# Weight operands of a decoder layer begin at 27 places in memory instead of one

## Chip, cores and metric

The kernel runs on one core of one Trainium2 chip. The metric is device time in microseconds (us) of one execution. A core has several engines that run side by side: TensorE (PE; its weight loads are listed apart as PEld) multiplies matrices, VectorE (DVE) and ScalarE (ACT) do elementwise work, GpSimd (POOL) does a little here, and SyncE (SP) issues the DMAs. They share the on-chip memory SBUF with 128 partitions; the matmuls accumulate in PSUM.

## What is computed

One layer of a decoder, 1024 tokens, width 1024, all in float32:

```python
mods = silu_c @ w_ada[l] + b_ada[l]          # shift, scale, gate for three sub-layers
h = modulate(x, sh1, sc1)
y = swiglu(h, ffn1_w_gate[l], ffn1_w_up[l], ffn1_w_down[l])
x = layer_norm(ALPHA * x + (1 + g1) * (MACARON * y), ln1_g[l], ln1_b[l])
h = modulate(x, sh2, sc2)
y = token_mix(h, w_in[l], b_forget[l], swa_sinks[l], grp_gain[l], w_out[l])
x = layer_norm(ALPHA * x + (1 + g2) * y, ln2_g[l], ln2_b[l])
h = modulate(x, sh3, sc3)
y = swiglu(h, ffn2_w_gate[l], ffn2_w_up[l], ffn2_w_down[l])
x = layer_norm(ALPHA * x + (1 + g3) * (MACARON * y), ln3_g[l], ln3_b[l])
```

`swiglu` is `(silu(h @ w_gate) * (h @ w_up)) @ w_down` with an inner width of 2816. `token_mix` projects `h`, runs eight heads of sliding-window attention (window 128) and eight heads of forgetting attention (a cumulative sum of log forget gates is added to the scores), normalises both groups and projects back.

## The kernel before

A float32 operand is split into a high part and the rest (`split`, lines 100 to 102: a copy on ACT, a subtraction on DVE), and a product is three matmuls: high x high, high x rest, rest x high (`mm3`, lines 106 to 108). Nearly all PE work runs through these lines, 128 x 128 weights against up to 512 moving columns. The large products are computed by blocks with seven products instead of eight (a Strassen-like scheme), so DVE also forms sums and differences of blocks.

The work goes in this order: a start that modulates the input and begins the first FFN (`start_ffn1`); gate and up products of the first FFN (`gate_up`, eleven groups `g` of 2 x 7 products, in the class `Seven`); its down projection (`down`, seven products of eleven steps each); value, query and key projections; sliding-window attention, then forgetting attention, with projections as filler between; the output projection; the second FFN with `gate_up` and `down` again. Vector work on the modulation vectors (`ada_mul`, line 122) is spread through the first `gate_up`.

SBUF is given out by rings. A ring has a tag, a number of slots and a slot size; a tile takes a free slot, and its first writer waits until the last reader of the slot's former tile has finished. Before the change:

```python
RING = dict(h=(14, 8192), z=(4, 4096), q=(4, 4096), w=(6, 4096), u=(6, 2048), t=(7, 2048), b=(2, 4096))
```

The number pairs are slots and bytes per partition. The tiles of concern:

- `w`: split operands, high part and rest side by side, 4096 bytes. In `gate_up` and in the q/k projection they are the weights (stationary operand); in `down` and in the output projection they are the moving operand, and in the later products of `down` both. Each value tile and each projected q/k tile is also put together in a `w` tile before it is stored.
- `t`: short-lived sums, 2048 bytes: the partial results of the seven products, the sums `s1`, `s2` of weight blocks (lines 265 and 266), the `T2` sums of `down` (line 416), the split scores of both attentions, and the small arrays of the cumulative sum (lines 815 to 842).
- `upper`: a constant 128 x 128 triangle, loaded once at the start (line 650) and used by a single matmul, the cumulative sum over tokens (line 826).
- `u`: pieces of weights as they are loaded; `h`, `z`, `q`: larger operands.

Every slot of these rings is a whole number of 512 bytes long. The weight slices in a tile are 512 bytes long, the rows of a moving operand 2048 bytes. The second value projection is different: its weights (`wv_load`, line 772 on ACT and 773 on DVE) lie as slices of 328 columns, 1312 bytes, in an `h` tile and are the moving operand of 328-wide matmuls; the first value projection has slices of 320 columns, 1280 bytes.

The program is written in one order; a planner then orders each engine's instructions by that priority, by their dependencies and by the slots that are free, before the program runs. Each engine carries out its list strictly in order, and so does the DMA queue of SP.

Of the kernel before, what the change touches and what calls it, by code (L numbers as in the profile page):

```python
# [14 lines left out]
P = 128  # L15
# [22 lines left out]
RATIO2 = 0.3  # L38


RING = dict(h=(14, 8192), z=(4, 4096), q=(4, 4096), w=(6, 4096), u=(6, 2048), t=(7, 2048), b=(2, 4096))
BANK = dict(mm=3, o=1, y=2, tp=2)


# [1 line left out]
def layer_kernel(ctx, tc, xT, x, c, adaT, adab, wg1, wu1, wd1, wqk, wv1, wv2, bf, sinks,  # L46
# [5 lines left out]
    V, A, G, T, DMA = nc.vector, nc.scalar, nc.gpsimd, nc.tensor, nc.sync  # L52

    sb = ctx.enter_context(tc.tile_pool(name="sb", bufs=1))
# [4 lines left out]
    def mk(pool, shape, dt, tag, bufs):  # L59
        uid[0] += 1  # L60
        return pool.tile(shape, dt, tag=tag, name=f"{tag}_{uid[0]}", bufs=bufs)

    def st(tag, shape, dt=F32):
        assert 4 * math.prod(shape[1:]) <= RING[tag][1], (tag, shape)
        return mk(sb, shape, dt, tag, RING[tag][0])

    def const(shape, name, dt=F32):
        return sb.tile(shape, dt, tag=name, name=name, bufs=1)
# [4 lines left out]
    def psum(tag):  # L73
        return mk(ps, [P, HT], F32, tag, BANK[tag])
# [3 lines left out]


    ident = const([P, P], "ident")  # L80
    upper = const([P, P], "upper")
    cmask = const([P, P], "cmask")
    ones = const([P, P], "ones")
    nhalf = const([P, 8], "nhalf")
# [28 lines left out]
    def htiles():  # L113

        return [st("h", [P, 4, HT], F32R) for _ in range(2)]

    silu = st("b", [P, D])

    def ada_mul(w, j):
# [5 lines left out]
    def ada_block(m, d):  # L125
        j = m * KD + d
        w = st("q", [P, D])
        DMA.dma_start(w, adaT[j * P:(j + 1) * P, :])
        ada_mul(w, j)
# [517 lines left out]
    ops1, wo1, a1 = start_ffn1()  # L647

    DMA.dma_start(ident, consts[0])
    DMA.dma_start(upper, consts[1])  # L650
    DMA.dma_start(cmask, consts[2])
    DMA.dma_start(lnc, lncol)
    DMA.dma_start(gaincol, gain)
# [132 lines left out]
    for hf in range(2):  # L786
        if hf:
            wpre.append(weight_all(wqk, order[0], "w"))
        for pz, (w, ncol) in enumerate(((wva, NV1), (wvb, NV2))):
            for k in range(4):  # L790
                t = hf * 4 + k
                p = psum("y" if hf + pz == 0 and k < 2 else "mm")
# [19 lines left out]
    def flat(t):  # L812
        return t.rearrange("p a b -> p (a b)")
# [8 lines left out]
    V.tensor_tensor(fl, fl, fa, ALU.subtract)  # L822
    V.tensor_scalar(fz, fz, 0.0, None, op0=ALU.min)
    V.tensor_tensor(fl, fz, fl, ALU.subtract)
    pc = psum("tp")
    T.matmul(pc[:, :64], upper, flat(fl), start=True, stop=True)
    V.tensor_copy(flat(fw), pc[:, :64])
# [649 lines left out]
```

## Time and profile before

| | |
|---|---|
| median of two runs | 1780.41 us (1780.15 to 1780.66) |
| the profiled execution | 1779.88 us |
| span from the first to the last instruction in it | 1778.1 us |
| mean granted TensorE clock | 0.997 |
| PE / DVE / ACT busy | 98% / 85% / 44% of the span |
| DMA | 303.44 MB, 171 GB/s over the span |

A page of the profile lists busy time per engine, the span in 40 slices, the DMA queues, the chain of work that ended last, and the costliest groups of instructions. A group's row reads: source line, engine, operation, what it writes and reads by tile names (buffer numbers left out), shapes and count; then busy time in us and the mean of one in ns; then how long the engine sat idle just before these instructions and what ended that. A row of the timeline has the start in us, the duration, the engine, the line and the operation. Matmuls overlap in the pipeline, so a matmul's own duration is longer than its share of PE; the distance between two starts is what one costs in an unbroken run. In a table of stretches each row gives the stretch, its length, then busy time and instruction count of PE, PEld, DVE, ACT and POOL as far as they occur, the granted clock, the DMA share and GB/s.

### The profile page before, as it was taken

Reading aid. Unit: us, or ns where it says so; the run is one execution under the profiler, and the core shown is the slowest. Engines: PE = TensorE matmul, PEld = TensorE weight load, DVE = VectorE, ACT = ScalarE, POOL = GpSimd, SP = SyncE. Lnnn points to the kernel's source line nnn. Section 1 sums busy time; section 2 is a strip of 40 time slices with the busy share of each in tenths; the row PEclk is TensorE's granted clock in tenths of the full one; section 3 lists DMA queues with packets and bytes.
Section 4 is the critical chain, followed back from the end, with each engine's and each line's share of the span. In section 5 each row is a group of like instructions: output and inputs, shape, how many; then the busy total and the mean of one; then the engine's idle time right before and its main releaser. Section 6 shows DMA issues by size and latency. Waiting matters only on the chain.

```text
span 1778.1 us, 23525 instructions
## 1 busy us (share of the span) xinstructions
PE 1739.8 (98%) x8114; PEld 1435.1 (81%) x8114; DVE 1510.3 (85%) x2748; ACT 782.6 (44%) x1492; POOL 21.9 (1%) x32
## 2 busy tenths in 40 slices
PE   6999999999999999999999999999999999999997
PEld 5788888888888889887787768788888888888885
DVE  7999999999895788267787987998887887899688
ACT  5433333333444453277666651643333333354472
POOL 0000000000000000000000000000000000000000
PEclk9999999999999999999999999999999999999999
DMA  9355555556944327655767863243233232593452
GB/s 367 115 192 196 181 201 192 177 185 222 331 145 142 109 87 239 205 155 169 214 202 226 238 218 137 84 142 125 90 132 105 95 106 96 209 318 102 136 166 78
DMA packets 147047, 303.44 MB, mean 171 GB/s; under 512 B 15384, under 2 KB 29296, under 8 KB 146928
## 3 DMA queue, kind: packets, MB, share of 16 engines
q1 hardware_dynamic: 146928, 301.94, 52.3%
q8 instruction: 64, 1.05, 0.3%
q14 instruction: 55, 0.45, 0.1%
HBM read 224.17 MB, written 77.71 MB: 170 GB/s over the span
## 4 chain that ended last, share of the span: by engine, by line
PE 87%; DVE 8%; ACT 3%; issue 1%; POOL 0%; DMA 0%; SPq 0%; POOLq 0%; ACTq 0%; DVEq 0%
PE y L106 12%; PE y L107 12%; PE y L108 12%; PE mm L108 9%; PE mm L107 9%; PE mm L106 9%; PE o L106 3%; PE o L108 3%; PE o L107 3%; PE tp L106 2%; PE tp L107 2%; PE tp L108 2%; DVE h L102 2%; PE tp L1166 2%; PE o L1174 1%
## 5 line engine op out<-in xcount | busy, mean ns | idle before, releaser
L101 ACT CAST w<-u 128x512 fp32r<-128x512 f32 x295 | 181.4, 621 | 359.7 <-PE y L108 137.5
L106 PE MATMUL y<-h,w 128*128 128x512 f32 x716 | 281.4, 393 | 0.3 <-ACT w L101 0.3
L107 PE MATMUL y<-h,w 128*128 128x512 f32 x716 | 280.3, 391 | 0.0
L108 PE MATMUL y<-h,w 128*128 128x512 f32 x716 | 280.1, 391 | 0.0
L106 PE MATMUL mm<-h,w 128*128 128x512 f32 x540 | 211.3, 392 | 16.5 <-ACT h L101 15.7
L102 DVE TENSOR_TENSOR w<-u,w 128x512 fp32r<-128x512 f32 x295 | 200.9, 686 | 21.2 <-ACT w L101 20.3
L107 PE MATMUL mm<-h,w 128*128 128x512 f32 x540 | 211.7, 393 | 0.0
L108 PE MATMUL mm<-h,w 128*128 128x512 f32 x540 | 211.1, 392 | 0.4 <-DVE w L102 0.4
L106 PEld LDWEIGHTS y<-h,w 128*128 128x128 f32 x716 | 134.6, 188 | 27.5 <-ACT w L101 1.1
L108 PEld LDWEIGHTS y<-h,w 128*128 128x128 f32 x716 | 134.5, 188 | 25.7
L107 PEld LDWEIGHTS y<-h,w 128*128 128x128 f32 x716 | 134.6, 188 | 25.7
L101 ACT CAST w<-t 128x512 fp32r<-128x512 f32 x106 | 65.6, 620 | 174.5 <-PE mm L108 70.8
L106 PEld LDWEIGHTS mm<-h,w 128*128 128x128 f32 x540 | 101.7, 188 | 38.8 <-ACT h L101 16.1
L107 PEld LDWEIGHTS mm<-h,w 128*128 128x128 f32 x540 | 102.1, 189 | 21.8 <-DVE h L102 0.8
L108 PEld LDWEIGHTS mm<-h,w 128*128 128x128 f32 x540 | 102.1, 189 | 21.9 <-DVE w L102 1.1
L101 ACT CAST z<-u 128x512 fp32r<-128x512 f32 x88 | 54.8, 622 | 103.8 <-PE y L108 79.9
L102 DVE TENSOR_TENSOR t<-tp,t 128x512 fp32r<-128x512 f32 (+1 forms) x126 | 72.8, 586 | 20.0 <-ACT t L101 18.9
L102 DVE TENSOR_TENSOR z<-u,z 128x512 fp32r<-128x512 f32 x88 | 59.9, 687 | 26.6 <-ACT z L101 26.6
L101 ACT CAST w<-h 128x512 fp32r<-128x512 f32 x111 | 68.5, 617 | 31.8 <-DMA h<-in_wd 11.6
L102 DVE TENSOR_TENSOR w<-h,w 128x512 fp32r<-128x512 f32 x111 | 76.1, 686 | 5.0 <-ACT w L101 4.9
L101 ACT CAST t<-tp 128x512 fp32r<-128x512 f32 (+1 forms) x126 | 62.5, 501 | 32.6 <-PE tp L1166 31.7
L102 DVE TENSOR_TENSOR w<-t,w 128x512 fp32r<-128x512 f32 x106 | 72.6, 688 | 1.3 <-ACT w L101 0.8
(349 smaller groups left out, 3907.7 us busy)
## 6 DMA issues: line engine op xcount, KB each, us to landing
u<-aT SPq DMA_DIRECT2D x154, 256.0 KB, 2.8
q<-in_adaT SPq DMA_DIRECT2D x56, 512.0 KB, 3.4
u<-in_wg SPq DMA_DIRECT2D x92, 256.0 KB, 3.3
u<-in_wu SPq DMA_DIRECT2D x90, 256.0 KB, 2.8
aT<-z SPq DMA_DIRECT2D x44, 512.0 KB, 3.2
h<-in_wd SPq DMA_DIRECT2D x88, 256.0 KB, 5.4
qkd<-w SPq DMA_DIRECT2D x26, 512.0 KB, 3.7
aT<-b SPq DMA_DIRECT2D x22, 512.0 KB, 4.0
```

The source lines that it names most:

```text
L101: A.copy(hi, src)
L102: V.tensor_tensor(lo, src, hi.bitcast(F32), ALU.subtract)
L106: T.matmul(o, lh, rh, start=start, stop=False, skip_group_check=more)
L107: T.matmul(o, lh, rl, start=False, stop=False, skip_group_check=more)
L108: T.matmul(o, ll, rh, start=False, stop=stop, skip_group_check=more)
L1166: T.transpose(pt[:, tok(i - q0)], sps[i][:, tok(j)], ident)
L1174: T.matmul(po[:, c0:], vt, ph[:, c0:], start=j == 0, stop=False)
```

## The change

- The slots of ring `w` become 416 bytes longer (4512), and each new `w` tile starts 16 bytes further in its slot than the one before, from 0 to 416 bytes, after which it begins again: 27 places.
- Ring `t` has six slots instead of seven.
- The constant `upper` no longer has a place of its own. It becomes a tile of ring `t`, loaded just before the matmul that uses it.

```diff
-RING = dict(h=(14, 8192), z=(4, 4096), q=(4, 4096), w=(6, 4096), u=(6, 2048), t=(7, 2048), b=(2, 4096))
+RING = dict(h=(14, 8192), z=(4, 4096), q=(4, 4096), w=(6, 4096 + 416), u=(6, 2048), t=(6, 2048), b=(2, 4096))
...
+    turn = [0]
+
     def st(tag, shape, dt=F32):
-        assert 4 * math.prod(shape[1:]) <= RING[tag][1], (tag, shape)
-        return mk(sb, shape, dt, tag, RING[tag][0])
+        n = math.prod(shape[1:])
+        assert 4 * n <= RING[tag][1], (tag, shape)
+        if tag != "w":
+            return mk(sb, shape, dt, tag, RING[tag][0])
+
+        w = mk(sb, [P, RING[tag][1] // 4], dt, tag, RING[tag][0])
+        o = 4 * (turn[0] % 27)
+        turn[0] += 1
+        w = w[:, o:o + n]
+        if len(shape) == 3:
+            return w.rearrange("p (a b) -> p a b", a=shape[1])
+        return w.rearrange("p (a b c) -> p a b c", a=shape[1], b=shape[2]) if len(shape) == 4 else w
...
-    upper = const([P, P], "upper")
...
-    DMA.dma_start(upper, consts[1])
...
     V.tensor_tensor(fl, fz, fl, ALU.subtract)
+    upper = st("t", [P, P])
+    DMA.dma_start(upper, consts[1])
     pc = psum("tp")
     T.matmul(pc[:, :64], upper, flat(fl), start=True, stop=True)
```

## The prediction

> **What bounds the kernel now.** I read the page first: how busy the engines are, and the chain that ended last.
>
> ```profile
> span 1778.1 us, 23525 instructions
> PE 1739.8 (98%) x8114; PEld 1435.1 (81%) x8114; DVE 1510.3 (85%) x2748; ACT 782.6 (44%) x1492; POOL 21.9 (1%) x32
> PE 87%; DVE 8%; ACT 3%; issue 1%; POOL 0%; DMA 0%; SPq 0%; POOLq 0%; ACTq 0%; DVEq 0%
> ```
>
> TensorE (PE) carries 87% of the chain, so almost nothing but its own pace and its own waits can move the end. A mean hides stages, so I took the busy time by stretches (length, then busy PE, PEld, DVE, ACT with instruction counts, granted clock, DMA), and PE's waits.
>
> ```profile
> 80.00:200.00 120.00, 120.00 (x530) 98.81 (x530) 117.95 (x195) 38.98 (x67) 0.00 (x0) 1.00 0.57 194
> 200.00:340.00 140.00, 140.00 (x620) 115.81 (x619) 137.16 (x227) 44.59 (x76) 0.00 (x0) 1.00 0.55 187
> 340.00:380.00 40.00, 40.00 (x178) 33.14 (x177) 38.75 (x65) 12.34 (x21) 0.00 (x0) 1.00 0.60 193
> ...
> 760.00:860.00 100.00, 98.98 (x533) 78.62 (x532) 75.01 (x216) 73.92 (x221) 0.96 (x1) 1.00 0.58 167
> 860.00:1060.00 200.00, 193.92 (x1033) 154.40 (x1032) 171.21 (x438) 129.79 (x288) 1.65 (x1) 1.00 0.74 219
> 1060.00:1140.00 80.00, 78.78 (x379) 64.22 (x377) 65.04 (x109) 27.09 (x42) 6.74 (x9) 1.00 0.39 136
> ```
>
> ```profile
> PE mm L106 <- ACT h L101: 15.7, 2, 13.0
> PE y L106 <- ACT w L101: 1.8, 2, 1.5
> PE mm L1141 <- DVE s_mneg L1144: 1.6, 3, 0.6
> ```
>
> See two things. In the gate/up products of the first FFN (80 to 380 us) PE never idles, at full clock, and VectorE (DVE) is busy 293.9 of 300 us: it has 6.1 us to spare and would be the next bound. In the attention and output projection (760 to 1140) PE idles 1.0 + 6.1 + 1.2 = 8.3 us. The 13.0 us wait is the kernel's start; the other waits are for operands just computed, 1.8 us or less a pair.
>
> **The pace of PE.** Start times of matmuls inside unbroken runs, 512, 320 and 328 columns wide:
>
> ```profile
> 299.62 0.39 PE L107 MATMUL mm<-h,w 128*128 128x512 f32 x1
> ...
> 305.97 0.39 PE L108 MATMUL o<-h,w 128*128 128x512 f32 x1
> ```
> ```profile
> 699.82 0.31 PE L107 MATMUL mm<-h,h 128*128 128x320 f32 x1
> ...
> 705.98 0.31 PE L107 MATMUL mm<-h,h 128*128 128x320 f32 x1
> ```
> ```profile
> 711.77 0.31 PE L107 MATMUL mm<-h,h 128*128 128x328 f32 x1
> ...
> 719.84 0.31 PE L107 MATMUL mm<-h,h 128*128 128x328 f32 x1
> ```
>
> The first pair spans 28 steps: 6.35/28 = 226.8 ns a matmul. The second spans 42: 6.16/42 = 146.7 ns. The third spans 54: 8.07/54 = 149.4 ns. Widths 512 and 320 differ by 80.1 ns over 192 columns, 0.417 ns a column; that leaves 226.8 - 512 x 0.417 = 13.2 ns per matmul that doesn't grow with the columns. This 13.2 ns is all that a better place in memory could win, if operands at like places are what costs it.
>
> **Part 1, the places of `w`.** Nothing is computed differently: a `w` tile starts 0 to 416 bytes later in its slot, and the slots lie 4512 instead of 4096 bytes apart. How many instructions touch these tiles (busy PE, PEld, DVE, ACT, with counts):
>
> ```profile
> 0.00:1778.10 1778.10, 1431.14 (x6084) 1137.37 (x6084) 370.44 (x554) 331.62 (x554) 1.00 0.53 171
> ```
>
> So 6084 of 8114 matmuls read `w`, as weights or as the moving operand, and 554 operations each of DVE and ScalarE (ACT) write or read it. Do places matter to PE? Before, all slots of the wide rings and all slices in them lie a multiple of 256 bytes apart, with one exception: the slices of the second value projection are 328 x 4 = 1312 bytes apart, so its moving operand begins at 0, 288, 64, 352, 128 and 416 bytes past a multiple of 512, while its weights stay put. These are six of the 27 places, all multiples of 32. On the line through the other two widths a 328-wide matmul takes 13.2 + 328 x 0.417 = 150.0 ns; measured 149.4. So places 32 bytes apart change the pace by -0.6 ns, not by 13. 14 of the 27 places are multiples of 32. The other 13 are odd multiples of 16, and no row shows one; nor does a row show weights, rather than the moving operand, at other places. I bound an operation at an odd place by the whole of the 13.2 ns, gained or lost, and take 0 ns, being nearest to the 328-wide row; over 6084 matmuls the row's own -0.6 ns would be -3.7 us, which I keep for the range.
>
> DVE and ACT: the same 320- and 328-wide slices are written by these two groups (min/median/max).
>
> ```profile
> L773 DVE TENSOR_TENSOR h<-u,h x16: 489/491/501, 652.1 to 674.8; 128x320 fp32r<-128x320 f32 x8, 128x328 fp32r<-128x328 f32 x8
> ```
> ```profile
> L772 ACT CAST h<-u x16: 447/460/469, 651.2 to 674.3; 128x320 fp32r<-128x320 f32 x8, 128x328 fp32r<-128x328 f32 x8
> ```
> ```profile
> L102 DVE TENSOR_TENSOR w<-u,w 128x512 fp32r<-128x512 f32 x295 | 200.9, 686 | 21.2 <-ACT w L101 20.3
> ```
>
> A DVE column costs (686 - 491)/192 = 1.0 ns, so eight more columns are 8 of the 12 ns between least and most; 4 ns are left for the place. In the one stretch where DVE is near its limit about 110 operations write `w` (300 us / 38.1 us a group of 14 products x 14 splits): 110 x 4 ns = 0.4 us of the 6.1 spare. Cost 0. If that cover were gone, all of it would show.
>
> **Part 2, six slots for `t`.** A slot fewer matters only where seven sums live at once. Followed from first writer to last reader through the timeline, at most five live at once in the gate/up and attention stages, so six slots hold them with no new wait. Seven live only in the third product of the down projection, where DVE makes the T2 sums (L416) ahead of their splits:
>
> ```profile
> 1605.95 0.68 DVE L416 TENSOR_TENSOR t<-h,h 128x512 f32<-128x512 f32 x1
> ...
> 1614.38 0.68 DVE L416 TENSOR_TENSOR t<-h 128x512 f32<-128x512 f32 x1
> ...
> 1618.58 1.29 DVE L102 TENSOR_TENSOR w<-t,w 128x512 fp32r<-128x512 f32 x2
> ...
> 1631.83 0.69 DVE L102 TENSOR_TENSOR w<-t,w 128x512 fp32r<-128x512 f32 x1
> ```
> ```profile
> 1615.32 0.39 PE L106 MATMUL tp<-w,z 128*128 128x512 f32 x1
> ```
>
> The last T2 sum starts at 1614.4, its split at 1631.8, and six others are alive between. With six slots about ten sums (five in each down projection) must start 2 to 5.5 us later, after a split. What queues behind is DVE's own next split, and PE waits for that. PE starts this product at 1615.3 and needs a group each 12 x 226.8 = 2.7 us, so the fifth group at 1626.2; its split is done at about 1619.2. The lead is 7 us, more than 5.5. DVE has the same work in another order: 0, at worst the few us by which a lead is used up.
>
> **Part 3, the matrix `upper`.** Its 64 KB load leaves the start (0.42 us of the SP queue) and comes back just before the cumulative sum.
>
> ```profile
> L826 PE MATMUL tp<-t,upper x2: 217/245/273, 727.7 to 727.7; 128*128 128x64 f32 x2
> L650 SPq DMA_DIRECT2D upper<-in_consts x1: 423/423/423, 40.9 to 40.9; - x1
> DMA to landing us min/median/max: 5.3/5.3/5.3
> ```
> ```profile
> 723.11 0.36 SPq L801 DMA_DIRECT2D vd<-w  x1
> 723.83 1.08 SPq L558 DMA_DIRECT2D u<-in_wqk  x2
> 726.05 1.33 SPq L889 DMA_DIRECT2D h<-vd  x2
> ```
>
> The start gains nothing: PE's 13 us there wait for the first splits, long before 40.9. At 727.7 a late load would hold PE, with the q/k projection queued behind. The load waits for no data, only for a `t` slot, few of which are in use there, and SP's issues leave gaps (one ends at 723.47, the next begins at 723.83). If it is issued early it costs 0; if only with the chain at 724 to 726, at a landing of 5.3 us, 1.6 to 3.6 us. I take 0.5 us, near the early end, and keep 5.3 for the range. It pushes weight loads (L558) and `h<-vd` back by 0.42 us, hidden behind running matmuls.
>
> **Sum.** 1779.88 us (the profiled execution; span 1778.1 plus 1.8 around it) + 0 + 0 + 0.5 = 1780.4; the median of the runs is 0.5 above that execution, so **1781 us**. Below: -3.7 for places, -8.3 if another order of the attention stage removed all of PE's idle time: 1768. Above: +5.3 for `upper`, +8.3 if that idle time doubled: 1795. That order may shift at all, since slots decide when an instruction may be placed.
>
> **Rivals.**
> A, *the like places are the 13.2 ns.* For it: every matmul with `w` pays it, and all these operands begin at like places. Against: the 328-wide row. If odd places alone escape, 13/27 x 6084 x 13.2 ns = 39 us: 1742. If all do, 80 us: 1700. The Trainium skill ("TensorE: Matmul & The Clock Gate", section "Back-to-back issue gap") gives a warm gap of N/2.4 + 2.5 ns, 215.8 for 512 columns; the trace's 226.8 disagrees by 11 ns, and were the place the reason for all of it, that page would give 67 us less, about 1714. Chance 5%.
> B, *odd places cost PE a second fixed part.* The same 39 us the other way: 1820. Nothing in the trace speaks for it. The skill ("SBUF — State Buffer", section "Specifications (TRN2)") has lines of 16 bytes; by that page a start at a whole line touches no further line, which speaks against B, and no run shows it yet. Chance 3%.
> C, *DVE becomes the bound in the first FFN.* It decides once the 110 splits take 55 ns more each (6.1 us / 110), or 110 ns if only half do. If an odd place doubled the column time of a split (512 x 1.0 ns), 53 x 512 ns = 27 us less 6.1 spare: +21, 1802. Against: the 4 ns above. Chance 4%.
> D, *`upper` comes late and holds PE*: +2 to 5 us, 1783 to 1786, inside the range. Chance 6%.
> That the change doesn't do what it says: the longer slots shift by 416 bytes of their own, so places still spread; no case of its own.
>
> **How the numbers follow.** My forecast has 82%, A 5, B 3, C 4, D 6. The range 1768 to 1795 holds the forecast and D, less a few for a reordering larger than assumed: 8 in 10 or somewhat more. Faster by over 2% (about what a measurement of this kernel can tell from no change) is A: 0.05. Slower by over 2% is B, with a little for the unforeseen: 0.04. Within: 0.91.
>
> **What would show it.** Right: 512-wide matmuls still 226 to 227 ns apart in the gate/up stages; `w` splits still near 686 ns; no PE wait on `t`; L416 sums later by a few us with PE unbroken at 1615; at most a short PE gap at L826. Wrong: steps in the spacing that differ from one `w` tile to the next (A or B), DVE at 100% with PE gaps between 80 and 380 us (C), or a new wait of PE for `upper` (D).

## The result and the profile after

The changed kernel takes **1806.55 us** (1805.92 to 1807.18, two runs) against 1780.41: ratio 1.0147, 95% interval 1.013 to 1.0163. It is slower by 26 us, which is less than 2% and many times the uncertainty. The forecast was 1781 with a range up to 1795, so it failed. The profiled execution took 1805.92 us, its span 1804.0.

The page of the changed kernel: span, busy time and the chain that ended last; then the costliest group of matmuls with `w` and DVE's part of the splits (lines are 11 or 12 higher than before: L106 is now L117, L102 is L113).

```profile
span 1804.0 us, 23499 instructions
PE 1766.5 (98%) x8114; PEld 1435.6 (80%) x8114; DVE 1513.0 (84%) x2748; ACT 782.8 (43%) x1492; POOL 21.9 (1%) x32
PE 90%; DVE 6%; ACT 2%; issue 1%; DMA 0%; POOL 0%; SPq 0%; POOLq 0%; ACTq 0%; DVEq 0%
L113 DVE TENSOR_TENSOR w<-u,w 128x512 fp32r<-128x512 f32 x295 | 201.0, 686 | 30.4 <-ACT w L112 29.7
L117 PE MATMUL y<-h,w 128*128 128x512 f32 x716 | 283.7, 396 | 1.3 <-ACT w L112 1.3
```

The same 8114 matmuls keep PE busy for 1766.5 us instead of 1739.8: 26.7 us more, where the whole span grew by 25.9. DVE (1513.0 for 1510.3), ACT (782.8 for 782.6) and weight loads (1435.6 for 1435.1) do not move, and the `w` split still takes 686 ns. PE's share of the chain rises from 87% to 90%. So PE isn't kept waiting; it is slower at the same work. Its longest waits in the table of waits say the same:

```profile
PE mm L117 <- ACT h L112: 14.8, 2, 12.7
PE y L117 <- ACT w L112: 2.8, 2, 1.5
PE mm L117 <- DVE z L650: 1.2, 1, 1.2
```

The kernel's start is still the first, and no new kind of wait stands behind it. Where PE never idles, its pace can be read as a count of matmuls in a stretch. The same stretch of the first gate/up stage as before (length, then busy PE, PEld, DVE, ACT with counts, granted clock, DMA):

```profile
80.00:200.00 120.00, 120.00 (x518) 96.74 (x518) 115.36 (x189) 37.80 (x66) 0.00 (x0) 1.00 0.55 187
200.00:340.00 140.00, 140.00 (x605) 113.14 (x605) 134.68 (x221) 43.93 (x74) 0.00 (x0) 1.00 0.53 180
340.00:380.00 40.00, 40.00 (x175) 32.48 (x174) 38.41 (x63) 12.21 (x20) 0.00 (x0) 1.00 0.58 182
```

PE is busy without a gap in both kernels, at a granted clock of 1.00 in both. But 140 us hold 605 matmuls instead of 620, and 120 us hold 518 instead of 530: 226.8 x 620/605 = 232.4 ns and 226.8 x 530/518 = 232.1 ns a matmul. DVE has more room, not less: 288.5 us of 300 instead of 293.9. From the timeline of the changed kernel, a place where one `w` tile follows another:

```profile
200.06 0.40 PE L117 MATMUL mm<-h,w 128*128 128x512 f32 x1
...
201.92 0.39 PE L119 MATMUL mm<-h,w 128*128 128x512 f32 x1
202.15 0.39 PE L117 MATMUL y<-h,w 128*128 128x512 f32 x1
...
203.29 0.39 PE L119 MATMUL y<-h,w 128*128 128x512 f32 x1
```

Eight steps in the product that writes `mm` take 1.86 us, 232.5 ns each; five in the next one, which reads other `w` tiles, take 1.14 us, 228.0 ns each. That is the sign that the prediction set down for "wrong": the spacing changes from one `w` tile to the next.

Two landmarks split the 26 us, the cumulative sum and the last operation of the output projection (first the second of them before, then both after):

```profile
L968 DVE SCALAR_TENSOR_TENSOR h<-y,rB,h x16: 699/748/752, 1085.2 to 1130.2; 128x512 f32<-128x512 f32 x16
```
```profile
L838 PE MATMUL tp<-t,t x2: 217/246/274, 740.0 to 740.1; 128*128 128x64 f32 x2
L980 DVE SCALAR_TENSOR_TENSOR h<-y,rB,h x16: 700/748/751, 1098.1 to 1143.3; 128x512 f32<-128x512 f32 x16
```

Up to the cumulative sum 727.7 became 740.0, so +12.3. From there to 1130.2 and 1143.3 it is 402.5 and 403.3, +0.8: attention with its projections and the output projection lose almost nothing. The rest, 1130.2 to 1778.1 and 1143.3 to 1804.0, is 647.9 and 660.7, +12.8. The loss sits in the two FFNs, where PE hardly ever waits. The stretch between, before and then after:

```profile
727.70:1130.20 402.50, 394.91 (x2039) 317.32 (x2038) 313.26 (x776) 232.94 (x553) 7.93 (x9) 1.00 0.64 192
740.00:1143.30 403.30, 396.63 (x2039) 318.47 (x2039) 313.29 (x777) 233.23 (x553) 7.94 (x9) 1.00 0.63 191
```

PE is busy 1.7 us longer there too, for the same 2039 matmuls, and idles 6.7 us instead of 7.6: half of the loss of this stretch is taken from its waits. It is small from the start, since only 792 of its matmuls read `w`, and their steps were mixed before the change already (by the start times 229.6 ns in the mean where two 512-wide ones follow each other, 231.2 after).

### The profile page after: what moved, and what is told of

It is laid out like the page before. It is cut to its first block, busy times and chain, and to the rows that moved or that the text cites. A ratio compares the mean times of both kernels' runs of the same rounds, so it can differ in the third digit from the quotient of the medians.

```text
span 1804.0 us, 23499 instructions
## 1 busy us (share of the span) xinstructions
PE 1766.5 (98%) x8114; PEld 1435.6 (80%) x8114; DVE 1513.0 (84%) x2748; ACT 782.8 (43%) x1492; POOL 21.9 (1%) x32
## 4 chain that ended last, share of the span: by engine, by line
PE 90%; DVE 6%; ACT 2%; issue 1%; DMA 0%; POOL 0%; SPq 0%; POOLq 0%; ACTq 0%; DVEq 0%
PE y L117 12%; PE y L118 12%; PE y L119 12%; PE mm L119 10%; PE mm L118 10%; PE mm L117 10%; PE o L117 3%; PE o L119 3%; PE o L118 3%; PE tp L119 2%; PE tp L118 2%; PE tp L117 2%; PE tp L1178 1%; DVE h L113 1%; PE o L1186 1%; PE o L1187 1%
## 5 line engine op out<-in xcount | busy, mean ns | idle before, releaser
L117 PE MATMUL y<-h,w 128*128 128x512 f32 x716 | 283.7, 396 | 1.3 <-ACT w L112 1.3
L117 PE MATMUL mm<-h,w 128*128 128x512 f32 x540 | 213.9, 397 | 16.6 <-ACT h L112 14.8
L113 DVE TENSOR_TENSOR w<-u,w 128x512 fp32r<-128x512 f32 x295 | 201.0, 686 | 30.4 <-ACT w L112 29.7
L118 PE MATMUL mm<-h,w 128*128 128x512 f32 x540 | 213.6, 396 | 0.0
L119 PE MATMUL mm<-h,w 128*128 128x512 f32 x540 | 213.2, 395 | 0.0
L117 PEld LDWEIGHTS y<-h,w 128*128 128x128 f32 x716 | 134.6, 188 | 30.6 <-ACT w L112 1.7
L117 PEld LDWEIGHTS mm<-h,w 128*128 128x128 f32 x540 | 101.8, 189 | 41.3 <-ACT h L112 15.2
L113 DVE TENSOR_TENSOR z<-u,z 128x512 fp32r<-128x512 f32 x88 | 60.0, 687 | 35.3 <-ACT z L112 34.2
L113 DVE TENSOR_TENSOR t<-tp,t 128x512 fp32r<-128x512 f32 (+1 forms) x126 | 72.7, 586 | 19.3 <-ACT t L112 18.3
L113 DVE TENSOR_TENSOR w<-h,w 128x512 fp32r<-128x512 f32 x111 | 75.9, 684 | 2.0 <-ACT w L112 1.9
L113 DVE TENSOR_TENSOR w<-t,w 128x512 fp32r<-128x512 f32 x106 | 72.6, 688 | 2.4 <-ACT w L112 2.1
```

Of the source, the lines that this page charges most:

```text
L113: V.tensor_tensor(lo, src, hi.bitcast(F32), ALU.subtract)
L117: T.matmul(o, lh, rh, start=start, stop=False, skip_group_check=more)
L118: T.matmul(o, lh, rl, start=False, stop=False, skip_group_check=more)
L119: T.matmul(o, ll, rh, start=False, stop=stop, skip_group_check=more)
```

## The experiments

All times stand against runs of the kernel before on the same chip, 1780.69 to 1781.16 us in the median. Where no ratio is given, the time is that of one execution, and what the run says rests on the steps in its trace. "By the start times" means the mean distance between two starts, read to the nanosecond. "Place" means how many bytes further in its slot a tile begins; in the kernel before all slots of the wide rings lie at one place modulo 512 bytes, so the distance between the places of weights and moving operand is 0 there, or a multiple of 256.

In the runs that move `w`, its slots are 4352 bytes long (17 x 256) instead of 4512, and, but for the run with multiples of 256, the offset is `o = 4 * turn[0]`, without a step from tile to tile. The cuts from their edits, which stand against the changed kernel, leave these two lines out where they are the same again.

**Parts 2 and 3 alone.** Six `t` slots and the late `upper`, with `w` as before.

```diff
-RING = dict(h=(14, 8192), z=(4, 4096), q=(4, 4096), w=(6, 4096), u=(6, 2048), t=(7, 2048), b=(2, 4096))
+RING = dict(h=(14, 8192), z=(4, 4096), q=(4, 4096), w=(6, 4096), u=(6, 2048), t=(6, 2048), b=(2, 4096))
...
-    upper = const([P, P], "upper")
...
-    DMA.dma_start(upper, consts[1])
...
+    upper = st("t", [P, P])
+    DMA.dma_start(upper, consts[1])
```

> Six slots for t and upper as a tile of t, as in the changed kernel; w tiles as before (slots of 4096 bytes, no shift). Theory P (the place of weights against the moving operand sets the fixed part of a matmul): 1780 to 1783 us, 512-wide matmuls 226.8 ns apart. Theory O (the slot less, the late load and the order that follows cost the 26 us): 1800 to 1807 us, with PE waits that the kernel before does not have.

Measured: 1779.76 us, ratio 0.9994 (0.9985 to 1.0004). Both parts together cost nothing. What is left for the 26 us is the places of `w`.

**One place for each group.** In both `gate_up` stages the weight tiles of a group of 14 products share one place, which changes from group to group; elsewhere the place is 0.

```diff
-RING = dict(h=(14, 8192), z=(4, 4096), q=(4, 4096), w=(6, 4096 + 416), u=(6, 2048), t=(6, 2048), b=(2, 4096))
+RING = dict(h=(14, 8192), z=(4, 4096), q=(4, 4096), w=(6, 4096 + 256), u=(6, 2048), t=(6, 2048), b=(2, 4096))
...
-        o = 4 * (turn[0] % 27)
-        turn[0] += 1
+        o = 4 * turn[0]
...
+        g = c // 2
+        turn[0] = g if w is wg1 or w is wu1 else (0, 11, 12, 13, 14, 15, 1, 3, 6, 9, 11)[g]
...
+        turn[0] = 0
         return res
```

> Slots of w 4352 bytes long (17 x 256); every w tile at the start of its slot, but for the gate/up weights: group g of the first FFN has all its weights g x 16 bytes in, the groups of the second 0, 176, 192, 208, 224, 240, 16, 48, 96, 144, 176. One place per group of 168 matmuls. P: spacing differs from group to group, 226.8 at 0, 228 to 231 at 144, 176, 192 and 240, 232 to 234 at the others (as the changed kernel shows on average by place); about 1798 us. Theory T (what costs is that neighbouring tiles begin at different places): 226.8 in all groups, about 1781 us. O: about 1806 us with 226.8 in all groups.

Measured: 1797.81 us. Stretches of 36 us inside single groups, at places 16, 32, 64 and 96 in the first FFN, then 240, again 16, 48 and 176 in the second:

```profile
68.00:104.00 36.00, 36.00 (x156) 29.03 (x155) 34.89 (x59) 12.57 (x22) 0.00 (x0) 1.00 0.58 198
106.00:142.00 36.00, 36.00 (x157) 28.77 (x156) 34.68 (x56) 10.89 (x20) 0.00 (x0) 1.00 0.52 185
185.00:221.00 36.00, 36.00 (x156) 28.99 (x155) 34.84 (x59) 11.37 (x19) 0.00 (x0) 1.00 0.53 179
264.00:300.00 36.00, 36.00 (x156) 28.87 (x155) 34.14 (x56) 11.73 (x20) 0.00 (x0) 1.00 0.49 172
1342.00:1378.00 36.00, 36.00 (x160) 29.84 (x159) 28.95 (x46) 11.60 (x19) 0.00 (x0) 1.00 0.30 103
1380.00:1416.00 36.00, 36.00 (x161) 29.81 (x160) 29.02 (x46) 11.57 (x19) 0.00 (x0) 1.00 0.29 102
1418.00:1454.00 36.00, 36.00 (x156) 29.31 (x155) 28.01 (x44) 11.50 (x19) 0.00 (x0) 1.00 0.29 103
1536.00:1572.00 36.00, 36.00 (x158) 29.39 (x157) 28.05 (x45) 14.32 (x23) 0.00 (x0) 1.00 0.69 236
```

The kernel before has 160 matmuls in the first of these stretches and 161 in the fifth. By the start times a matmul takes 233 to 234 ns at 16, 32, 48, 64 and 96 bytes in the first FFN, and 230 at 176 and 227 at 240 in the second. Two places forecast at 228 to 231 cost the full amount: 144 bytes 233.4 and 192 bytes 233.3 ns. Multiples of 32 cost as much as odd multiples of 16. The loss is about 6.6 ns a matmul, half of the 13.2 by which the prediction had priced rival B. One thing doesn't fit a plain rule: 16 bytes costs 6.6 ns in the first FFN and nothing in the second (x156 and x161).

**Everything moved together.** The kernel before with a longer constant ahead of the rings, so all their slots begin 32 bytes later and all distances stay.

```diff
-    nhalf = const([P, 8], "nhalf")
+    nhalf = const([P, 16], "nhalf")
```

> The kernel before, with one small constant 32 bytes longer ahead of the rings: all operands start 32 bytes later, none against another. P, if only the difference of the two operands' places counts: 226.8 ns, 1780 us. Theory L (the start of each operand within a line of 64 bytes counts): another spacing, 2 to 7 ns away, so 1765 or 1792 to 1825 us.

Measured: 1780.42 us, and 620 matmuls again between 200 and 340 us:

```profile
200.00:340.00 140.00, 140.00 (x620) 115.82 (x619) 137.16 (x227) 44.59 (x76) 0.00 (x0) 1.00 0.54 187
```

At 32 bytes the absolute place costs nothing; the same 32 bytes between `w` and the other operand cost 6.6 ns.

**Multiples of 256.** The changed kernel with two places, 0 and 256, in turn, and slots of 4352 bytes.

```diff
-        o = 4 * (turn[0] % 27)
+        o = 64 * (turn[0] % 2)
```

> The changed kernel, but weight operand tiles begin in turn at 0 and 256 bytes in their slots instead of 27 places. Theory P (what counts is the distance between the places of weights and moving operand, counted within 256 bytes): 512-wide matmuls 226.7 ns apart everywhere, 620 of them between 200 and 340 us, time 1778 to 1783 us. Rival F (the distance counts within 512 bytes or more): the tiles at 256 run at 230 to 234 ns, a mean of 229 to 230 ns, 610 to 615 matmuls between 200 and 340 us, time 1790 to 1797 us. Rival V (any change of place from one tile to the next costs, whatever the distance): 231 to 233 ns throughout, about 605 matmuls, time 1800 to 1808 us.

Measured: 1780.64 us, ratio 0.9997 (0.9987 to 1.0006). Two stretches of it:

```profile
200.00:340.00 140.00, 140.00 (x620) 115.83 (x619) 136.83 (x226) 44.55 (x76) 0.00 (x0) 1.00 0.53 187
480.00:540.00 60.00, 60.00 (x266) 49.71 (x265) 57.61 (x96) 28.68 (x50) 0.00 (x0) 1.00 0.52 171
```

The old pace is back, although places still change from tile to tile. The turn itself costs nothing, and a distance of 256 bytes is as good as 0. In the changed kernel, distances that are no multiple of 256 come from the turn and from the slots, which lie 4512 = 17 x 256 + 160 bytes apart; this run takes out both, and they were not tried apart.

**All `w` at 48.** No turn; every `w` tile 48 bytes in.

```diff
-    turn = [0]
+    turn = [3]
...
-        o = 4 * (turn[0] % 27)
-        turn[0] += 1
+        o = 4 * turn[0]
```

> As the changed kernel, but w slots of 4352 bytes and every w tile 48 bytes in: no place changes from tile to tile. P (a relative place costs a fixed 6.6 ns a matmul, whatever the neighbours): 233.3 ns for weights at 48 and for the moving operand at 48 (208 the other way round), 226.8 only where both operands are w tiles (540 matmuls); 5544 x 6.6 ns = 37 us more, 1814 to 1819 us. T (changes of place from one tile to the next cost): 1781 us.

Measured: 1812.29 us, ratio 1.0177 (1.016 to 1.0194), slightly under what was expected. First two stretches of it, then the kernel before in three stretches of the down projections and the second gate/up:

```profile
200.00:340.00 140.00, 140.00 (x603) 113.81 (x602) 134.13 (x219) 43.75 (x73) 0.00 (x0) 1.00 0.51 180
490.00:550.00 60.00, 60.00 (x259) 48.32 (x258) 55.60 (x92) 27.33 (x48) 0.00 (x0) 1.00 0.53 171
```
```profile
490.00:550.00 60.00, 60.00 (x266) 49.67 (x266) 54.51 (x91) 28.00 (x50) 0.00 (x0) 1.00 0.44 132
1300.00:1540.00 240.00, 240.00 (x1060) 198.73 (x1059) 196.72 (x304) 79.21 (x131) 0.00 (x0) 1.00 0.31 103
1610.00:1670.00 60.00, 60.00 (x267) 49.67 (x266) 45.20 (x74) 26.68 (x48) 0.00 (x0) 1.00 0.37 109
```

The gate/up products, where `w` is the weights, and the down products, where it is the moving operand (x259; x266 before), both run 233.3 ns apart. But where both operands are `w` tiles, so their distance is 0, the spacing is 231 to 233, not the 226.8 that a rule of distance alone gives.

**Is that a matter of place 48 itself?** Only in the fifth down product, where both operands are `w` tiles, both begin 48 bytes in.

```diff
-                a, w = (st(q, [P, 2, HT], F32R) for q in (ring[0], ring[-1]))
+                turn[0] = 3 if ring == "w4" else 0
+                a, w = (st(q, [P, 2, HT], F32R) for q in (ring[0], "w"))
+                turn[0] = 0
...
+            if i == 4:
+                return "w4"
```

> w slots of 4352 bytes, all w tiles at the start of the slot, but for the fifth product of each down projection, where both operands are w tiles and both 48 bytes in: no difference, entered from 226.7 ns. R (only the difference counts, and what e5_all_at_48 showed there, 233.3 ns, was carried over from the products before): 226.7 ns. A (a place that is an odd multiple of 16 costs by itself): 231 to 233.3 ns. Total 1780 to 1782 us.

Measured: 1782.1 us. The timeline in an earlier down product, at 0, and in the fifth:

```profile
499.78 0.39 PE L116 MATMUL mm<-w,z 128*128 128x512 f32 x1
...
517.91 0.39 PE L118 MATMUL y<-w,z 128*128 128x512 f32 x1
...
571.73 0.39 PE L118 MATMUL y<-w,w 128*128 128x512 f32 x1
...
589.98 0.39 PE L116 MATMUL tp<-w,w 128*128 128x512 f32 x1
```

The first pair spans 80 steps, 18.13/80 = 226.6 ns; the second 79, 18.25/79 = 231.0. So the same place for both isn't always free: 48 bytes cost 4.4 ns with no distance at all. Distance alone explains the 6.6 ns of 32 bytes, where moving everything was free, but not those of 48.

**All `w` at 240**, the place that had cost nothing above (`turn = [15]` in the edit of place 48).

> As e5_all_at_48, with 240 bytes instead of 48. P: weights at 240 cost nothing (226.8 in the sweep), the moving operand of down at 240 is a difference of 16, where the sweep showed 233.3 in one FFN and 226.8 in the other; so 1780 to 1788 us. T: 1781 us. A theory that any place but the original one costs: 1814 to 1819 us.

Measured: 1792.79 us, above what was expected.

```profile
200.00:340.00 140.00, 140.00 (x620) 115.86 (x619) 136.86 (x227) 44.63 (x76) 0.00 (x0) 1.00 0.54 186
490.00:550.00 60.00, 60.00 (x259) 48.26 (x258) 52.78 (x87) 28.02 (x49) 0.00 (x0) 1.00 0.41 127
1300.00:1540.00 240.00, 240.00 (x1053) 197.18 (x1052) 193.40 (x300) 77.18 (x127) 0.00 (x0) 1.00 0.29 103
1610.00:1670.00 60.00, 60.00 (x255) 48.29 (x254) 49.12 (x81) 26.11 (x46) 0.00 (x0) 1.00 0.30 93
```

Against x620, x266, x1060 and x267 in the kernel before: 240 is free in the first gate/up, costs 6.6 ns in the first down projection, 1.6 in the second gate/up, and 10 in the second down projection (60 us for 255 instead of 267). As weights it is nearly free, as the moving operand it isn't; and two stages with the same operands differ. Where both operands are `w` tiles and both 240 bytes in, a step is 231.1 ns by the start times: the 4.4 ns of 48 bytes once more.

**Why did the 328-wide row mislead?** First the kernel before with the first value projection's 320-wide slices spaced as the second's, at six places.

```diff
-            w = st("h", [P, 2, nk, ncol], F32R)
+            w = st("h", [P, 2, nk, NV2], F32R)[:, :, :, :ncol]
```

> The kernel before, with the 320-wide slices of the first value projection laid 1312 bytes apart instead of 1280, so its moving operand starts at 0, 288, 64, 352, 128, 416 against the weights. P, if places work as at 512 columns: 146.7 ns becomes about 151 (the mean of 0, 6, 2.5, 6.5, 6, 7 more). If a moving operand at places 32 bytes apart costs nothing, as the prediction read from the 328-wide row: 146 to 147 ns. Total time 1780 to 1782 us either way (192 matmuls).

Measured: 1779.83 us, first and last of 96 matmuls in the timeline:

```profile
661.33 0.30 PE L106 MATMUL y<-h,h 128*128 128x320 f32 x1
...
675.27 0.31 PE L108 MATMUL mm<-h,h 128*128 128x320 f32 x1
```

13.94/95 = 146.7 ns, as before. Next, the same place at both widths: 64 bytes for the moving operand of the first four down products (512 columns) and for the 320-wide slices, weights at 0.

```diff
+                turn[0] = 4 if ring == "zw" else 0
                 a, w = (st(q, [P, 2, HT], F32R) for q in (ring[0], ring[-1]))
+                turn[0] = 0
...
-            w = st("h", [P, 2, nk, ncol], F32R)
+            if ncol == NV1:
+                w = st("h", [P, 2 * nk * ncol + 16], F32R)[:, 16:]
...
```

> w slots of 4352 bytes, all w tiles at the start of the slot, but for the moving operand of the first four products of each down projection, 64 bytes in; and the 320-wide slices of the first value projection all 64 bytes in, 1280 apart. P: the down products (1056 matmuls) go to 233.3 ns, +7 us, 1786 to 1789 us. For the 320-wide matmuls two theories of why the 328-wide row showed nothing: W (the width decides; at 320 columns no place costs): 146.7 ns. M (a place costs only when it stays the same from matmul to matmul, and the 328-wide slices changed it each time): 153.3 ns.

Measured: 1781.94 us, below what was expected. The down products go from x266 to x264 in 60 us (228.9 ns by the start times), the 320-wide ones stay at 146.7.

```profile
490.00:550.00 60.00, 60.00 (x264) 49.23 (x263) 53.54 (x89) 27.54 (x49) 0.00 (x0) 1.00 0.41 127
```

Last, 48 bytes: in the first four down products the high part at 0 and the rest 48 bytes out, and all of the 320-wide slices 48 bytes in.

```diff
-                a, w = (st(q, [P, 2, HT], F32R) for q in (ring[0], ring[-1]))
+                a = st(ring[0], [P, 2, HT], F32R)
+                if ring == "zw":
+                    w = st("w", [P, 2, HT + 12], F32R)[:, :, :HT]
+                else:
+                    w = st("w", [P, 2, HT], F32R)
...
-            w = st("h", [P, 2, nk, ncol], F32R)
+            if ncol == NV1:
+                w = st("h", [P, 2 * nk * ncol + 12], F32R)[:, 12:]
...
```

> w slots of 4352 bytes. In the first four products of each down projection the moving operand's high part starts 0 and its rest 48 bytes out of line with the weights, so the place changes at every matmul; the 320-wide slices of the first value projection all start 48 bytes in. M (a place costs only when it stays the same from matmul to matmul): the 1056 down matmuls 226.7 ns, the 320-wide ones 153.3 ns. W (the width decides, mixing does not help): down 228 to 234 ns, 320-wide 146.7 ns. Total 1780 to 1788 us.

Measured: 1790.5 us, above what was expected. The down stretch, and the first and last of 92 matmuls of the 320-wide kind:

```profile
490.00:550.00 60.00, 60.00 (x257) 47.76 (x256) 52.16 (x86) 27.55 (x49) 0.00 (x0) 1.00 0.40 125
```
```profile
665.50 0.31 PE L116 MATMUL y<-h,h 128*128 128x320 f32 x1
...
678.85 0.31 PE L117 MATMUL mm<-h,h 128*128 128x320 f32 x1
```

In one kernel, 0 and 48 bytes in turn cost a 512-wide matmul about 9 ns (x257 for x266; 235.5 ns by the start times), and 48 bytes cost a 320-wide one nothing (13.35/91 = 146.7). It also isn't a mix of places that protects the narrow ones: here all their slices share one place, and mixing makes the wide ones worse than 48 throughout (233.3). The narrower matmuls don't show the effect in their mean; the 328-wide row from which the prediction argued most likely could not have shown it. Their single steps do shift, and even out: by the start times they are 146 or 147 ns in the kernel before, 145 or 150 here, and 141 to 153 with six places. Only the moving operand was moved at 320 columns, not the weights.

**The identity matrix in line with the rings**, with parts 2 and 3: its place differs from that of the rings, and steps of 231 to 236 ns remain after transposes in the kernel before.

```diff
-    nhalf = const([P, 8], "nhalf")
+    nhalf = const([P, 32], "nhalf")
```

> e1_t6_upper with one small constant 96 bytes longer between the identity matrix and the rings, so the identity, too, lies at a multiple of 256 bytes from all operands. P: the transposes no longer leave the matmuls after them at 231 to 236 ns in the attention stage (some 500 matmuls, 4 to 8 ns each), so 2 to 4 us less, 1776 to 1779 us. If those come from something else: 1779 to 1782 us.

Measured: 1779.07 us, ratio 0.999 (0.9981 to 0.9999), and as many of the slow steps as before (between 760 and 1140 us, 456 of 230 ns or more after a 512-wide matmul, 461 in the kernel before), so its place isn't their cause. The ratio is not told apart from that of parts 2 and 3 alone (0.9994). No version beat the kernel before by more than this 0.1%, and in no run were unbroken 512-wide matmuls steadily faster than 226.7 ns.

## Why the prediction was wrong

**The step that failed** is in part 1: "take 0 ns, being nearest to the 328-wide row". The working was sound for 328 columns, and the value was carried to 512 columns, where 6084 matmuls read `w`. At 512 columns the places cost 0 to 10 ns, with 6.6 the commonest. In the first FFN the mean is 232.1 to 232.4 less 226.8, some 5.5 ns. The loss shows as 12.3 us up to the cumulative sum and 12.8 us in the second FFN; attention loses only 0.8, with few matmuls on `w` and half of their loss taken from waits. The term for places stood at 0 in the sum and at -3.7 in the range, on the wrong side: measured +26.

**The bound was drawn on one side.** The prediction itself bounded an odd place by 13.2 ns, gained or lost, and then kept only -3.7 of it in the range. Nothing had excluded the loss: no row showed weights at another place, or 512 columns at one. Even 4.3 ns over 6084 matmuls, well inside that bound, is the 26 us.

**The rivals.** B had the direction and the kind (PE, a fixed part more per matmul, steps that differ from tile to tile), with two errors: the cost is at multiples of 32 too, and it is half as large. They pull opposite ways, so that its 1820 lies only 13 us from 1806.55 partly by luck. The Trainium skill ("SBUF — State Buffer", section "Specifications (TRN2)") has lines of 16 bytes, and every place here starts at a whole line; the measured 6.6 ns shows that whole lines are not enough. The 215.8 ns that rival A took from the Trainium skill ("TensorE: Matmul & The Clock Gate", section "Back-to-back issue gap") is on that page the gap of a single isolated matmul, so the 11 ns measured nothing of places. A is contradicted: like places were the best seen, not the reason for the 13.2 ns. C did not happen: splits at 686 ns, and DVE with more room.

**What held.** `t` at 0: parts 2 and 3 together gave 0.9994. The way was the forecast one: in the second down projection of that run five of the eleven T2 sums start 2.4 to 7.2 us later against their splits (forecast 2 to 5.5), the splits keep their distances, and no step of PE there is longer than 228 ns. `upper` at 0.5: its matmul waited for nothing that can be seen, but the early case is not what happened. The load's row in the changed kernel, and the timeline around its matmul:

```profile
L836 SPq DMA_DIRECT2D t<-in_consts x1: 441/441/441, 736.6 to 736.6; - x1
DMA to landing us min/median/max: 3.2/3.2/3.2
```
```profile
739.80 0.39 PE L117 MATMUL y<-h,w 128*128 128x512 f32 x1
...
740.04 0.33 PE L838 MATMUL tp<-t,t 128*128 128x64 f32 x2
```

The load is issued at 736.6, which is 724.3 in the kernel before (12.3 us less): with the chain, as in the late case. At the 5.3 us that the prediction took for the landing it would have cost 736.6 + 5.3 - 740.0 = 1.9 us. It landed in 3.2 us, at 739.8, and its matmul starts at 740.04, 0.24 us after the one ahead of it, an ordinary step. So the forecast of a small cost held by the luck of a faster landing, with some 0.2 us between the landing and the matmul.

**What stays open.** The mean paces run from 226.7 to 236.6 ns, with 233.3 the commonest, and which one a pair of places gets depends also on the stage: 16 bytes in the two FFNs, 240 in the two down projections. That the reading of the next weights meets the stream of the moving operand in memory would suit a cost that comes from both sides. No run was made for it, but the one with all `w` at 48 bears on it. In the last two products of its down projections, groups of matmuls with both operands in an `h` tile, at place 0, take turns with groups on `w` tiles. The last matmul of a group on `h` takes 232 to 233 ns to the next start in all 12 cases where the next weights lie in a `w` tile, the one ahead of it 226 to 227. With all `w` at 240, which as weights was nearly free, that last one takes 226 to 227 in all 12. So a step depends on the place of the next weights too, and not on the operands of one matmul alone; by what way is not shown. Nor was it settled why 320 columns escape.

## What to carry to other kernels

Where 512-wide matmuls run without a gap, begin weights and moving operands a multiple of 256 bytes apart, and look after any change of tile sizes or paddings whether that still holds; other distances cost 0 to 10 ns of 227 a matmul here. Nor move both together by 48 or 240 bytes (231 ns); by 32 it was free. A bound from a row of another width isn't a value: if the only evidence is for 328 columns and the work is 512 columns wide, both ends of the bound belong in the range. A change of PE's pace hides behind 98% busy at full clock; count the matmuls in the same stretch of both kernels.

## What the runs showed of the hardware that was not expected

- The pace of back-to-back 512-wide matmuls depends on where their operands begin in SBUF: 226.7 ns at distances of 0 and 256 bytes, 233.3 with `w` 48 bytes in, 235.5 when 0 and 48 alternate in the moving operand, at a granted clock of 1.00 throughout.
- It depends on the distance between the two operands (all moved by 32 bytes: 226.7; `w` alone by 32: 233) and, at least for 48 and 240 bytes, on the place itself (both at 48: 231.0; both at 240: 231.1).
- At 320 columns a moving operand 48 bytes in left the mean of 146.7 ns unchanged, in the very kernel in which 512 columns with 0 and 48 in turn paid 9 ns.
